# The last 512 columns of the second token tile as 384 and 128 instead of 256 and 256

## The chip, the cores and the metric

The kernel runs on one core of one Trainium2 chip. The core has a matrix engine (TensorE, in the profile PE, with its weight loads PEld), a vector engine (VectorE, DVE), a scalar engine (ScalarE, ACT), GpSimd (POOL) and a queue that issues transfers (SyncE, SP); each works through its own instructions in order and waits for the others by semaphores. The metric is the device time of one execution in microseconds, as the median of several runs.

## The reference

One layer of a decoder trunk on 256 tokens of width 2048, in float32. Cut to what the end of the kernel computes:

```python
h = rmsnorm(x, norm_mix_g)
u = h @ w_in                                   # 12 fields, 12288 columns
ya = b_g * causal_dwconv3(c_g * xa, conv_w) * silu(za)
...                                            # chunked gated recurrence -> yb
m = sigmoid(ga) * (ya @ w_a_out) + sigmoid(gb) * (yb @ w_b_out)
x = x + m @ w_o
gate = sigmoid(rmsnorm(x, ple_norm_g) @ w_ple_gate)
x = x + gate * (p @ w_ple_proj)
return rmsnorm(x, final_norm_g)
```

The change touches the last 512 columns of `gate`, the update of `x` by them, and the last norm.

## The kernel before

**Tiles.** The 256 tokens are two tiles of 128 (`NT` = 2, index `t`), which are the weights of the matmul (its 128 x 128 operand). The weight matrices of the layer are cut in groups of `CW` = 512 columns and stream through as the moving operand, so that one matmul gives 128 tokens x 512 columns, one PSUM bank. A float32 product is made of three: each operand is split into a rounded part and a rest (`hi` and `lo`, type fp32r), and `product` (line 954) issues hi x hi, hi x lo and lo x hi, each with its own weight load, all three added up in the same bank. Line 959 is the only matmul of all these products. The names in the profile: `xh`, `xl` are the two parts of the normed tokens, `whi`, `wlo` those of the weight matrix, `g` the PSUM bank.

**Order.** `steps` lists all groups of columns and, in each, the steps of K in pairs (`c`, two values of k each). For all groups but the last the loop over `steps[:last_group]` computes both tiles of tokens in step, into two banks. What follows a group on ScalarE, VectorE and GpSimd is a generator (an epilogue), and `advance` takes each active one a piece further after a step of the products.

**The last group.** The last 512 columns of the gate projection are done in another order (from line 1049): all 16 steps of K for the first tile of tokens, 512 columns wide; then all 16 for the second tile and columns 0 to 255 of the group; then all 16 for the second tile and columns 256 to 511. Each of the three has a bank of its own from a ring of four. The splits of the weights for all of them are kept, since they are used three times.

Behind each of the three comes its part of the last update:

- `last_half` (749) on 256 columns: sigmoid of the product times the token's scale on ScalarE (754), times the projection `pw` on VectorE (755), added to `x` (758), and square and sum over the columns on VectorE (759).
- `sums_so_far` (764), after the first of the two halves: adds what is known of the token's sum of squares (768, 772), so that only one number is left for the second half.
- `last_norm` (776), after the second: adds that number (779), takes the power -1/2 on GpSimd (780), scales all 2048 columns in pieces on ScalarE and VectorE (784, 786, 788) and stores them in three transfers on SP's queue (799).

For the first tile both halves come out of one product, and `ep_last` (801) runs all of this while the second tile's products go on. For the second tile `last_half` and `sums_so_far` of columns 0 to 255 lie beside the products of columns 256 to 511, and what follows these last products has nothing beside it.

Of the kernel before, what the change touches and what calls it, by code (L numbers as in the profile page):

```python
# [12 lines left out]
ALU = mybir.AluOpType  # L13
# [6 lines left out]
KT = D // P  # L20
# [3 lines left out]
CW = 512  # L24
PLE = 256
EPS = 1e-6

EARLY = {0: ((0, CW // 2), (CW // 2, CW), (CW, 2 * CW)), 1: ((0, CW), (CW, 2 * CW))}
WARM = (64,) * 51 + (CW,) * 3
LB_FLOOR = 1e-30  # L30
LB_MAX = 1.0 - 1e-6
# [15 lines left out]
def hybrid_kernel(ctx, tc, xT, x, pT, prm, gfin, masks, w_in, w_a, w_b, w_o, w_pg, w_pp, out):  # L47
# [24 lines left out]
    state = {"tmp": "tmp1"}  # L72
# [3 lines left out]
    def nm(s):  # L76
        uid[0] += 1
        return f"{s}_{uid[0]}"

    def t4(tag="t4", bufs=None):  # L80
        bufs = bufs or {"tmp1": 8, "tmp2": 5, "tmp3": 5}[state["tmp"]]
        return pools[state["tmp"]].tile([P, 1024], F32, tag=tag, bufs=bufs, name=nm(tag))

    def bank(tag):
        return ps.tile([P, CW], F32, tag=tag, bufs=4, name=nm(tag))
# [29 lines left out]
    def split(pos, c0=0, c1=2 * CW):  # L115
        w, g, c = stream[pos]
        src = load(pos)[:, pos % 2, :]

        pool, n = (pools["late"], 6) if (pos - state.get("late", len(steps))) % 10 < 6 and "late" in state else (wp, 4)
        if pos not in parts:  # L120
            parts[pos] = tuple(
                pool.tile([P, 2 * CW], F32R, tag=tag, bufs=n, name=nm(tag)) for tag in ("whi", "wlo")
            )
        hi, lo = parts[pos]
        s = slice(c0, c1)
        a = nc.scalar.activation(out=hi[:, s], in_=src[:, s], func=AF.Copy)  # L126
        v = nc.vector.tensor_tensor(  # L127
            out=lo[:, s], in0=src[:, s], in1=hi[:, s].bitcast(F32), op=ALU.subtract
        )
        state["splits"] = (a.ins, v.ins)  # L130
# [11 lines left out]
    active, done = [], 0  # L142
# [603 lines left out]
            d = xs[:, t, j * CW : (j + 1) * CW]  # L746
            nc.gpsimd.tensor_tensor(out=d, in0=d, in1=state["gfin"][:, j * CW : (j + 1) * CW], op=ALU.mult)

    def last_half(t, h, psum):

        xs, pw, ss, n = state["x"], state["pw", 3], state["ss3"], CW // 2
        gt = t4()[:, :n]
        d = xs[:, t, 3 * CW + h * n : 3 * CW + (h + 1) * n]
        nc.scalar.activation(out=gt, in_=psum, func=AF.Sigmoid, scale=state["rstd2"][:, t : t + 1])
        nc.vector.tensor_tensor(  # L755
            out=gt, in0=gt, in1=pw[:, t * CW + h * n : t * CW + (h + 1) * n], op=ALU.mult
        )
        nc.vector.tensor_tensor(out=d, in0=d, in1=gt, op=ALU.add)  # L758
        nc.vector.scalar_tensor_tensor(  # L759
            out=gt, in0=d, scalar=1.0 / D, in1=d, op0=ALU.mult, op1=ALU.mult,  # L760
            accum_out=ss[:, t * 6 + 3 + h : t * 6 + 4 + h],
        )

    def sums_so_far(t):

        tot = state["tot3", t] = sc(1, "tot3", 2)
        ss = state["ss3"]
        nc.vector.tensor_tensor(
            out=ss[:, t * 6 + 3 : t * 6 + 4], in0=ss[:, t * 6 + 3 : t * 6 + 4],
            in1=ss[:, t * 6 + 5 : t * 6 + 6], op=ALU.add,  # L770
        )
        nc.vector.tensor_reduce(
            out=tot, in_=ss[:, t * 6 : t * 6 + 4], axis=mybir.AxisListType.X, op=ALU.add
        )

    def last_norm(t):

        xs, r, tot = state["x"], sc(1, "r3", 2), state["tot3", t]
        nc.vector.tensor_tensor(out=tot, in0=tot, in1=state["ss3"][:, t * 6 + 4 : t * 6 + 5], op=ALU.add)
        nc.gpsimd.tensor_tensor(out=r, in0=tot, in1=mhalf[:, :1], op=ALU.pow)  # L780
        def scale(eng, c0, c1):
            d = xs[:, t, c0:c1]
            if eng is nc.scalar:
                nc.scalar.activation(out=d, in_=d, func=AF.Identity, scale=r)  # L784
            elif c0 < 3 * CW:
                nc.vector.tensor_scalar(out=d, in0=d, scalar1=r, scalar2=None, op0=ALU.mult)
            else:
                nc.vector.scalar_tensor_tensor(
                    out=d, in0=d, scalar=r, in1=state["gfin"][:, c0:c1], op0=ALU.mult, op1=ALU.mult
                )  # L790


        for pieces in (
            ((nc.vector, 768, 1024),), ((nc.scalar, 0, 512), (nc.vector, 512, 768)),
            ((nc.scalar, 1024, 1536), (nc.vector, 1536, 2048)),
        ):
            for eng, c0, c1 in pieces:
                scale(eng, c0, c1)
            nc.sync.dma_start(out=out[:, t, pieces[0][1] : c1], in_=xs[:, t, pieces[0][1] : c1])

    def ep_last(t, halves):

        last_half(t, 0, halves[0])
        sums_so_far(t)
        last_half(t, 1, halves[1])
        last_norm(t)
        yield

# [26 lines left out]
    wb = bank("s")  # L835
    for n in WARM:
        m = min(n, P)
# [104 lines left out]
    def advance():  # L942
        for e in list(active):
            step(e)
# [9 lines left out]
    def product(psum, op, k, t, hi, lo, first, last, which=(0, 1, 2)):  # L954

        oh, ol = (x[:, k, t * P : (t + 1) * P] for x in op)
        for n in which:
            a, b = ((oh, hi), (oh, lo), (ol, hi))[n]
            nc.tensor.matmul(psum, a, b, start=first and n == 0, stop=last and n == 2)  # L959

    psum = None
    for pos, (gi, c) in enumerate(steps[:last_group]):
        kind, j, w, g, opname = groups[gi]
# [9 lines left out]
        while done < min(pos + 1 + ahead(pos), len(steps)):  # L973

            for c0, c1 in EARLY.get(done, ((0, 2 * CW),)):
                if done == 0 and c0 % CW == 0:
# [22 lines left out]
        if c == 0:  # L999
            psum = [bank("s" if kind == "PP" and j > 1 else "g") for _ in range(NT)]  # L1000
        hi, lo = parts.pop(pos)
        for i in range(2):
            k = 2 * c + i
            for c0, c1 in EARLY[0][:2] if pos == 0 and i == 0 else ((0, CW),):
                s = slice(i * CW + c0, i * CW + c1)
# [41 lines left out]


    nlast = len(steps) - last_group
    for t, halves in ((0, (0, 1)), (1, (0,)), (1, (1,))):  # L1050
        bk, n = bank("g"), CW // 2
        for c in range(nlast):
            if done < len(steps):
                split(done)
                done += 1
            hi, lo = parts[last_group + c]
            for i in range(2):
                k = 2 * c + i
                s = slice(i * CW + halves[0] * n, i * CW + (halves[-1] + 1) * n)
                product(bk[:, : len(halves) * n], state["x1T"], k, t, hi[:, s], lo[:, s], k == 0, k == KT - 1)  # L1060
            if c % 2:
                advance()
        if t == 0:
            active.append(ep_last(t, [bk[:, h * n : (h + 1) * n] for h in halves]))
        else:
            last_half(t, halves[0], bk[:, :n])
            if halves[0] == 0:
                sums_so_far(t)
    last_norm(1)
    finish()  # L1070
# [74 lines left out]
```

## Time and profile before

| | us |
|---|---|
| median of 3 runs | 824.12 |
| lowest and highest | 823.97, 825.27 |
| the profiled execution, its own time | 824.47 |
| its span, first to last instruction | 822.7 |
| mean granted TensorE clock in it | 0.997 |

A row of a timeline is: start and length in us, engine, line, operation, the names of what it writes and reads, shapes, the count where rows are merged, and in brackets how long the engine stood idle before it and what ended that. In the groups by line, after the bar stand the busy time in us, the mean length of one in ns, and the idle time before. A matmul's record is longer than the distance to the next, because matmuls are pipelined; the distance from start to start is what one of them holds the engine.

### The profile page before, as it was taken

How to read it: one execution, taken by the hardware profiler on the slowest of the kernel's cores; microseconds unless marked ns; L12 is line 12 of the kernel's file. 1: busy time of each engine (PE TensorE's matmuls, PEld its weight loads, DVE VectorE, ACT ScalarE, POOL GpSimd, SP SyncE). 2: the span in 40 equal slices, each digit the busy share in tenths (PEclk: the TensorE clock that was granted, in tenths of full speed). 3: DMA queues.
4: the chain of work that ended last, by engine and by line, in shares of the span. 5: the costliest groups of instructions: out<-in, count | busy, mean ns of one | idle time of the engine just before them, and what ended most of it. 6: DMA issues, size and time to landing. Idle time of an engine off the chain costs nothing.

```text
span 822.7 us, 10783 instructions
## 1 busy us (share of the span) xinstructions
PE 813.4 (99%) x4235; PEld 676.0 (82%) x4236; DVE 531.1 (65%) x619; ACT 433.1 (53%) x559; POOL 90.6 (11%) x74
## 2 busy tenths in 40 slices
PE   9999999999999999999999999999999999999996
PEld 7888888888888888888888888888888888888885
DVE  5747698967766588877645546545545656679733
ACT  7666465565564565466443443544444455566522
POOL 1000045300000064200001001000100000001210
PEclk9999999999999999999999999999999999999998
DMA  9979656648776565748556755756755788887802
GB/s 339 368 271 340 222 188 209 214 155 253 259 230 229 198 205 165 246 153 294 198 184 184 264 189 173 252 205 205 239 182 195 253 278 275 314 291 279 301 0 104
DMA packets 41524, 187.27 MB, mean 228 GB/s; under 512 B 4736, under 2 KB 14208, under 8 KB 24320
## 3 DMA queue, kind: packets, MB, share of 16 engines
q1 hardware_dynamic: 41328, 186.31, 66.2%
q8 instruction: 33, 0.54, 0.3%
q10 hardware_dynamic: 144, 0.26, 0.1%
q14 instruction: 19, 0.16, 0.1%
HBM read 172.92 MB, written 13.63 MB: 227 GB/s over the span
## 4 chain that ended last, share of the span: by engine, by line
PE 97%; issue 1%; DMA 0%; DVE 0%; ACT 0%; ACTq 0%; POOLq 0%; POOL 0%
PE g L959 95%; PE s L959 1%; PE s L391 1%; DMA raw<-in_w_pp 0%; PE s L524 0%; PE s L547 0%; PE s L548 0%; PE s L546 0%; DVE t L755 0%; ACT xs L784 0%; DVE t L759 0%; DVE xs L758 0%; ACTq L1140 0%; POOLq L1140 0%; POOL r L780 0%
## 5 line engine op out<-in xcount | busy, mean ns | idle before, releaser
L127 DVE TENSOR_TENSOR wlo<-raw,whi 128x1024 fp32r<-128x1024 f32 (+1 forms) x295 | 368.0, 1252 | 252.1 <-ACT whi L126 251.5
L126 ACT ACTIVATE whi<-raw 128x1024 fp32r<-128x1024 f32 (+1 forms) x295 | 307.8, 1050 | 331.7 <-PE g L959 293.3
L959 PE MATMUL g<-whi,xl 128*128 128x512 f32 (+1 forms) x912 | 351.4, 385 | 0.0
L959 PE MATMUL g<-wlo,xh 128*128 128x512 f32 (+1 forms) x912 | 351.4, 385 | 0.0
L959 PE MATMUL g<-whi,xh 128*128 128x512 f32 (+1 forms) x912 | 351.2, 386 | 0.0
L959 PEld LDWEIGHTS g<-whi,xh 128*128 128x128 f32 x912 | 171.3, 188 | 34.4
L959 PEld LDWEIGHTS g<-whi,xl 128*128 128x128 f32 x912 | 171.3, 188 | 34.4
L959 PEld LDWEIGHTS g<-wlo,xh 128*128 128x128 f32 x912 | 171.3, 188 | 34.1
L959 PE MATMUL g<-whi,mh 128*128 128x512 f32 x128 | 49.8, 390 | 0.0
L959 PE MATMUL g<-wlo,mh 128*128 128x512 f32 x128 | 49.6, 389 | 0.0
L959 PE MATMUL g<-whi,ml 128*128 128x512 f32 x128 | 49.6, 390 | 0.0
L679 POOL TENSOR_TENSOR t<-ga,gb 128x512 f32<-128x512 f32 x6 | 10.6, 1792 | 198.3 <-DVE gb L674 198.3
L959 PE MATMUL g<-whi,yaTh 128*128 128x512 f32 (+1 forms) x74 | 28.3, 389 | 0.1
L959 PEld LDWEIGHTS g<-whi,mh 128*128 128x128 f32 x128 | 24.0, 188 | 5.2 <-ACT mh L685 0.3
L959 PEld LDWEIGHTS g<-whi,ml 128*128 128x128 f32 x128 | 23.9, 188 | 5.2 <-DVE ml L686 0.2
L959 PEld LDWEIGHTS g<-wlo,mh 128*128 128x128 f32 x128 | 24.0, 188 | 5.0
L959 PE MATMUL g<-whi,yaTl 128*128 128x512 f32 (+1 forms) x74 | 27.9, 384 | 0.0
L445 POOL TENSOR_TENSOR t<-b 128x512 f32<-128x512 f32 x10 | 20.4, 2037 | 68.5 <-DMA t<-turn 41.0
L959 PE MATMUL g<-wlo,yaTh 128*128 128x512 f32 (+1 forms) x74 | 27.9, 383 | 0.0
L959 PE MATMUL g<-whi,ybTh 128*128 128x512 f32 x64 | 24.9, 389 | 0.0
L959 PE MATMUL g<-wlo,ybTh 128*128 128x512 f32 x64 | 24.9, 389 | 0.0
L959 PE MATMUL g<-whi,ybTl 128*128 128x512 f32 x64 | 24.9, 389 | 0.0
(156 smaller groups left out, 518.2 us busy)
## 6 DMA issues: line engine op xcount, KB each, us to landing
raw<-in_w_in SPq DMA_DIRECT2D x85, 1024.0 KB, 5.0
raw<-in_w_o SPq DMA_DIRECT2D x16, 1024.0 KB, 5.6
raw<-in_w_pg SPq DMA_DIRECT2D x16, 1024.0 KB, 6.0
raw<-in_w_in SPq DMA_DIRECT2D x22, 512.0 KB, 7.9
turn<-t SPq DMA_DIRECT2D x72, 128.0 KB, 2.6
t<-turn SPq DMA_DIRECT2D x18, 512.0 KB, 5.3
raw<-in_w_a SPq DMA_DIRECT2D x8, 1024.0 KB, 5.3
raw<-in_w_b SPq DMA_DIRECT2D x8, 1024.0 KB, 5.2
```

What stands on the lines that cost most here:

```text
L126: a = nc.scalar.activation(out=hi[:, s], in_=src[:, s], func=AF.Copy)
L127: v = nc.vector.tensor_tensor(out=lo[:, s], in0=src[:, s], in1=hi[:, s].bitcast(F32), op=ALU.subtract)
L391: nc.tensor.matmul(heads(bk)[r, h, c if at is None else slice(at, at + 32)], key(h)[:, r], query(h)[:, c], start=True, stop=True, tile_pos ...
L445: nc.gpsimd.tensor_tensor(out=er, in0=br, in1=ref, op=ALU.subtract)
L679: (nc.vector if j == 3 else nc.gpsimd).tensor_tensor(out=spread(m, t), in0=blocks(ga[:, s]), in1=blocks(gb[:, s]), op=ALU.add)
L959: nc.tensor.matmul(psum, a, b, start=first and n == 0, stop=last and n == 2)
```

## The change

The constant `LAST` = 128 sets the width of the last part of the second tile. `last_half`, which took the number of a half, becomes `last_part`, which takes the columns `c0` to `c1`. The loop at the end takes the ranges of columns: 0 to 512 for the first tile, then 0 to 384 and 384 to 512 for the second. The first tile's update is still made in two halves of 256.

```diff
+LAST = 128
...
-    def last_half(t, h, psum):
+    def last_part(t, h, c0, c1, psum):

-        xs, pw, ss, n = state["x"], state["pw", 3], state["ss3"], CW // 2
-        gt = t4()[:, :n]
-        d = xs[:, t, 3 * CW + h * n : 3 * CW + (h + 1) * n]
+        xs, pw, ss = state["x"], state["pw", 3], state["ss3"]
+        gt = t4()[:, : c1 - c0]
+        d = xs[:, t, 3 * CW + c0 : 3 * CW + c1]
         nc.scalar.activation(out=gt, in_=psum, func=AF.Sigmoid, scale=state["rstd2"][:, t : t + 1])
         nc.vector.tensor_tensor(
-            out=gt, in0=gt, in1=pw[:, t * CW + h * n : t * CW + (h + 1) * n], op=ALU.mult
+            out=gt, in0=gt, in1=pw[:, t * CW + c0 : t * CW + c1], op=ALU.mult
         )
...
-    def ep_last(t, halves):
+    def ep_last(t, psum):

-        last_half(t, 0, halves[0])
+        last_part(t, 0, 0, CW // 2, psum[:, : CW // 2])
         sums_so_far(t)
-        last_half(t, 1, halves[1])
+        last_part(t, 1, CW // 2, CW, psum[:, CW // 2 :])
         last_norm(t)
...
-    for t, halves in ((0, (0, 1)), (1, (0,)), (1, (1,))):
-        bk, n = bank("g"), CW // 2
+    for t, c0, c1 in ((0, 0, CW), (1, 0, CW - LAST), (1, CW - LAST, CW)):
+        bk = bank("g")
...
-                s = slice(i * CW + halves[0] * n, i * CW + (halves[-1] + 1) * n)
-                product(bk[:, : len(halves) * n], state["x1T"], k, t, hi[:, s], lo[:, s], k == 0, k == KT - 1)
+                s = slice(i * CW + c0, i * CW + c1)
+                product(bk[:, : c1 - c0], state["x1T"], k, t, hi[:, s], lo[:, s], k == 0, k == KT - 1)
...
-            last_half(t, halves[0], bk[:, :n])
-            if halves[0] == 0:
+            last_part(t, int(c0 > 0), c0, c1, bk[:, : c1 - c0])
+            if c0 == 0:
                 sums_so_far(t)
```

More of the change, by code (lines that the diff above doesn't have):

```diff
@@ L1063, in hybrid_kernel @@
         if t == 0:
-            active.append(ep_last(t, [bk[:, h * n : (h + 1) * n] for h in halves]))
+            active.append(ep_last(t, bk))
         else:
-            last_half(t, halves[0], bk[:, :n])
-            if halves[0] == 0:
+            last_part(t, int(c0 > 0), c0, c1, bk[:, : c1 - c0])
+            if c0 == 0:
                 sums_so_far(t)
```

## The prediction

> **What bounds the kernel now.** I read the page's head first, then the chain that ended last.
>
> ```profile
> span 822.7 us, 10783 instructions
> PE 813.4 (99%) x4235; PEld 676.0 (82%) x4236; DVE 531.1 (65%) x619; ACT 433.1 (53%) x559; POOL 90.6 (11%) x74
> PE 97%; issue 1%; DMA 0%; DVE 0%; ACT 0%; ACTq 0%; POOLq 0%; POOL 0%
> 359.48 443.62 PE g L959 x1956
> ```
>
> TensorE is busy from end to end and makes up 97% of the chain (the last row is one piece of that chain: 1956 matmuls, all 512 columns wide, 443.62 us long). So one matmul of 512 columns holds TensorE for 443.62 / 1956 = 0.2268 us from its start to the start of the next. Whatever the change does to the sum of these gaps goes straight into the span; whatever it does behind the last matmul goes there too, because nothing else runs by then.
>
> Next I read the end of the span, engine by engine in equal stretches of the last product (columns after the stretch: PE, weight loads PEld, DVE, ACT, POOL, granted clock, DMA share, GB/s), and the timeline where the two 256-column halves of the second tile begin and end.
>
> ```profile
> 802.92:808.70 5.78, 5.78 (x50) 5.78 (x49) 3.81 (x14) 2.18 (x4) 0.55 (x1) 1.00 0.09 27
> 808.67:814.43 5.76, 5.76 (x50) 5.71 (x48) 1.60 (x6) 0.48 (x1) 0.00 (x0) 1.00 0.41 161
> 802.92 0.28 PE L959 MATMUL g<-whi,xh 128*128 128x256 f32 x1
> ...
> 808.67 0.28 PE L959 MATMUL g<-whi,xh 128*128 128x256 f32 x1
> ...
> 814.31 0.28 PE L959 MATMUL g<-whi,xl 128*128 128x256 f32 x1
> L959 PE MATMUL g<-whi,xl 128*128 128x512 f32 x880 | 342.4, 389 | 0.0
> L959 PE MATMUL g<-whi,xl 128*128 128x256 f32 x32 | 9.1, 283 | 0.0
> ```
>
> Each half is 48 matmuls (16 steps of K by three products). The first of the 96 starts at 802.92 and the last at 814.31, so one of 256 columns takes 11.39 / 95 = 0.1199 us. The granted clock is 1.00 in both stretches. The last two rows, from the groups by line with shapes kept apart, give the recorded length of one: 389 ns and 283 ns. These are longer than the gaps because a matmul's record includes its drain.
>
> Two things are to be seen. First, from 512 to 256 columns the gap falls by 0.1069 us, or 0.418 ns a column, and 0.013 us are left that don't depend on the width. Secondly, in these two stretches the weight loads are as busy as the matmuls (5.78 of 5.78, 5.71 of 5.76), while over the whole span they are at 82%: with 256 columns the loads have no air left.
>
> Last, the tail behind the last matmul:
>
> ```profile
> 808.93 0.48 ACT L754 ACTIVATE t<-g,r2r 128x256 f32<-128x256 f32 x1 [0.70 <-PE g L959]
> ...
> 814.63 0.47 ACT L754 ACTIVATE t<-g,r2r 128x256 f32<-128x256 f32 x1 [5.22 <-PE g L959]
> 815.13 0.42 DVE L755 TENSOR_TENSOR t<-t,pw 128x256 f32<-128x256 f32 x1 [3.95 <-ACT t L754]
> 815.59 0.42 DVE L758 TENSOR_TENSOR xs<-xs,t 128x256 f32<-128x256 f32 x1
> 816.05 0.42 DVE L759 SCALAR_TENSOR_TENSOR t<-xs 128x256 f32<-128x256 f32 x1
> 816.40 0.08 DVE L759 DVE_READ_ACCUMULATOR t<-xs 128x1 f32 x1
> 816.52 0.16 DVE L779 TENSOR_TENSOR tot<-tot,ss 128x1 f32<-128x1 f32 x1
> 816.76 0.55 POOL L780 TENSOR_TENSOR r<-tot,mhalf 128x1 f32<-128x1 f32 x1 [9.89 <-DVE tot L779]
> 817.34 1.34 ACT L784 ACTIVATE xs<-xs,r 128x512 f32<-128x512 f32 x2 [2.24 <-POOL r L780]
> ```
>
> Sigmoid, multiply, add, square and sum, total, power, scale, store: each waits for the one before (the first row is the sigmoid of the half before, at 808.93, which lies beside the matmuls). The first four work on the width of the last part. What stands from 816.52 on has fixed sizes and moves as a block with whatever comes before it.
>
> **The change part by part.**
>
> *The 48 wider matmuls.* They grow from 256 to 384 columns. No row shows 384; the bounds are 0.1199 and 0.2268 us, and by the straight line between them it is 0.1734. I take that, since every count of columns seen so far only adds its 0.418 ns. Cost: 48 x 0.0535 = +2.57 us.
>
> *The 48 narrower matmuls.* They shrink from 256 to 128 columns, and each still has a 128 x 128 weight load of its own (4236 loads to 4235 matmuls in the page's first rows), also the second product of a K step, which has the same tokens as weights as the first. No row shows a matmul of this split kind with fewer than 256 columns. The lowest price is the straight line: 0.013 + 128 x 0.000418 = 0.0665 us, which would give the 2.57 us back exactly. But these rows, the only places where two such loads follow each other with nothing in front of them, speak against it:
>
> ```profile
> 345.60 0.19 PEld L959 LDWEIGHTS g<-whi,xh 128*128 128x128 f32 x1
> 345.60 0.50 PE L959 MATMUL g<-whi,xh 128*128 128x512 f32 x1
> 345.71 0.19 PEld L959 LDWEIGHTS g<-wlo,xh 128*128 128x128 f32 x1
> 345.94 0.40 PE L959 MATMUL g<-wlo,xh 128*128 128x512 f32 x1
> ...
> 318.53 0.19 PEld L959 LDWEIGHTS g<-whi,xh 128*128 128x128 f32 x1
> 318.64 0.19 PEld L959 LDWEIGHTS g<-wlo,xh 128*128 128x128 f32 x1
> ```
>
> After another kind of work has ended, the second load starts 0.11 us after the first, and not sooner. The second matmul starts at 345.94, so by the gap of 0.2268 the first really began to stream at 345.71, 0.11 us after its load began and when the next load began. So a load holds its place for 0.11 us, and the next one begins when the matmul that uses it begins. With 256 columns (0.107 us of columns) this is just hidden; with 128 columns (0.053 us) it isn't, and the load sets the pace. A second kind of matmul with 128 columns and full weights bounds it too:
>
> ```profile
> 358.81 0.22 PE s L546 x2
> 359.03 0.22 PE s L547 x2
> 358.87 0.39 PE L547 MATMUL s<-v,aoff 128*128 128x128 f32 x2
> ```
>
> The plain f32 products of the recurrence are two records each, 0.22 us for both, 0.1115 us a record, each with a load of its own. So the narrow gap lies between 0.1115 (this row) and 0.1199 (own kind at 256 columns, as if nothing were saved by the narrower width). I take 0.115, between the two, nearer to the rows in which the load alone is seen.
>
> The stream from 802.92 to the end of the last record was 11.39 + 0.283 = 11.67 us. It becomes 48 x 0.1734 + 47 x 0.115 + 0.230 (the recorded length at 128 columns by the line through 389 and 283) = 8.32 + 5.41 + 0.23 = 13.96 us: **+2.28 us**, with +2.12 and +2.52 at the two ends.
>
> The Trainium skill, "TensorE: Matmul & The Clock Gate", section "LDWEIGHTS (loading the stationary operand)", speaks against this change too: a load takes its number of columns divided by 1.2 ns, 107 ns here, however many columns the matmul streams. The rows above agree (0.11). By the page's figure the stream would grow by 1.90 us in place of 2.28.
>
> *The tail.* The four width-bound steps go from 256 to 128 columns.
>
> ```profile
> L738 DVE TENSOR_TENSOR t<-t,pw 128x512 f32<-128x512 f32 x6 | 4.1, 692 | 4.2 <-ACT t L735 4.2
> L755 DVE TENSOR_TENSOR t<-t,pw 128x256 f32<-128x256 f32 x4 | 1.6, 426 | 14.0 <-ACT t L754 14.0
> L754 ACT ACTIVATE t<-g,r2r 128x256 f32<-128x256 f32 x4 | 1.8, 473 | 13.4 <-PE g L959 13.4
> L558 ACT ACTIVATE t<-s,r1r 128x128 f32<-128x128 f32 x16 | 5.6, 362 | 2.2 <-PE s L546 2.2
> L788 DVE SCALAR_TENSOR_TENSOR xs<-xs,r,gfin_t 128x512 f32<-128x512 f32 x2 | 1.5, 742 | 0.0
> ```
>
> VectorE: (692 - 426) / 256 = 1.04 ns a column, so 0.133 us less for each of three instructions, 0.40 us. ScalarE: 473 to 362 ns, 0.11 us. Together **-0.51 us**. The bounds are close: a VectorE instruction on one column (L779, 0.16) against one of 256 (0.42) gives 1.02 ns a column, so -0.50; the steeper line from L759 to L788 (742 against 421 ns) gives -0.59.
>
> *What moves and costs nothing.* The same sigmoid, multiply, add and square on the first part are half as wide again and start later, at 802.92 + 8.3 + drain = about 811.4 rather than 808.93. ScalarE needs some 0.58 us, VectorE three times 0.56 and the two small sums 0.35, so they are done at about 814.1. What hides them is the second part's matmuls; VectorE is wanted again at 816.9 + 0.4 = 817.3. Were the narrow matmuls as cheap as 0.0665 us, VectorE would be wanted at 815.0, still 0.9 us later. The count of matmuls, loads, banks and stores stays; no wait is added, nothing goes past another instruction on SP's or POOL's queue; the three stores of the second tile move with the scale that they wait for.
>
> *The sum.* +2.28 - 0.51 = +1.77 us, against the profiled execution's 824.47 us (its span of 822.7 and 1.8 around it): 826.24. That execution was 0.35 above the median of 824.12, so on the median: **825.9 us**, +0.21%. With both ends: +2.12 - 0.59 = +1.5 to +2.52 - 0.50 = +2.0, so 825.6 to 826.1, or 825.3 to 826.5 with the scatter of the runs shown.
>
> **The rivals.**
>
> *Narrow products fall to the plain f32 rate.* The f32 products above need 0.223 us for 128 columns (two records), that is 1.74 ns a column, while the split kind has 0.44 at 512 columns. No row shows that the split kind keeps its rate below 256 columns; that no part of this kernel goes narrower with it leaves the case open. If a narrow product is worked at the f32 rate, whatever the reason, the stream is 8.32 + 47 x 0.223 + 0.39 (length of such a pair) = 19.19 us, +7.52; less 0.51, +7.0: 831.1 us, +0.85%. Against it: the recorded kind is the same with the same load, and at 256 columns no step is seen. Chance 0.27.
>
> *The load hides after all (not slower).* If the next load could be started as early as wanted, the narrow gap is 0.0665 us, the stream 11.68 us, +0.01, and only the tail's gain stays: -0.5 us, 823.6. It decides from a load that takes its place for less than 0.067 us. For it speaks one row:
>
> ```profile
> 317.24 1.25 PEld L391 LDWEIGHTS s<-X 128*32 128x32 f32 x128 [0.35 <-issue]
> ```
>
> Loads of 32 columns follow each other every 0.010 us there, or 0.04 for 128 columns, so loading isn't slow in itself. Against it: those go to four separate strips of the array, while full loads keep 0.11 us wherever they are seen. Chance 0.10.
>
> *Loads overlap in part.* A load's record is 0.19 us long and the next starts 0.11 us after, so two are under way at once; with short matmuls in between the overlap could grow. Halfway between 0.0665 and 0.1115, a gap of 0.089 gives 8.32 + 4.18 + 0.23 = 12.73, +1.06; less 0.51, +0.55: 824.7. The same page of the Trainium skill, section "Back-to-back issue gap", has a stream of load and matmul pairs at about 81 ns for 128 columns, which would give +0.69 - 0.51 = +0.18, or 824.3. Its figure beside that for 512 columns is 131 ns, and the trace disagrees (226.8), so I give this little weight. Chance 0.07.
>
> **How the numbers follow.** Forecast 0.56, f32 rate 0.27, hidden load 0.10, partial overlap 0.07. The predicted time is the forecast's, 825.9. The range runs from 825.0, below the forecast's own 825.3, up to 831.3, over the f32 case; it leaves out the two cheap cases, 0.17. A change within 0.2% (1.65 us, 822.5 to 825.8) is about what a measurement of this kernel can tell from none. The forecast lies at this line: of its 0.56 I count 0.35 above and 0.21 below. Slower 0.35 + 0.27 = 0.62; same 0.21 + 0.07 + 0.08 = 0.36; faster 0.02, should the hidden load meet a larger gain in the tail.
>
> **What would show it.** In the profile of the changed kernel: 48 matmuls of 384 columns 0.173 us apart; then 48 of 128 columns, 0.11 to 0.12 us apart with the weight loads as densely packed, 0.22 for the f32 rate (perhaps as 96 records), 0.067 for the hidden load. The sigmoid at the very end should be at 0.36 us and the VectorE instructions at 0.29. The prediction is wrong if the narrow gap is under 0.10 or over 0.13 us, if the wide gap isn't 0.173, or if VectorE is still at work on the first part when the last sigmoid is done.

## The result and the profile after

| | before | after |
|---|---|---|
| median of 14 runs, us | 824.25 | 826.07 |
| ratio of the times, 95% interval | | 1.0020 (1.0012 to 1.0029) |
| profiled execution, us | 824.47 | 826.07 |
| its span, us | 822.7 | 824.3 |

The changed kernel is slower by 1.8 us between the medians (1.6 us between the profiled executions). The interval lies wholly above 1, and the ratio is just at the 0.2% line. One of the 14 executions of the changed kernel took 1181.36 us, at a mean granted clock of 0.653, and is left out of the ratio.

These are rows of the changed kernel's timeline, where the 384-column matmuls end and the 128-column ones begin and end (TensorE and its weight loads; the lines of the code have moved by one).

```profile
802.88 0.33 PE L960 MATMUL g<-whi,xh 128*128 128x384 f32 x1
...
811.05 0.33 PE L960 MATMUL g<-whi,xl 128*128 128x384 f32 x1
811.06 0.19 PEld L960 LDWEIGHTS g<-whi,xh 128*128 128x128 f32 x1
811.23 0.22 PE L960 MATMUL g<-whi,xh 128*128 128x128 f32 x1
811.23 0.19 PEld L960 LDWEIGHTS g<-wlo,xh 128*128 128x128 f32 x1
811.29 0.27 PE L960 MATMUL g<-wlo,xh 128*128 128x128 f32 x1
811.34 0.19 PEld L960 LDWEIGHTS g<-whi,xl 128*128 128x128 f32 x1
811.40 0.28 PE L960 MATMUL g<-whi,xl 128*128 128x128 f32 x1
...
816.42 0.28 PE L960 MATMUL g<-whi,xl 128*128 128x128 f32 x1
```

The wide matmuls are (811.05 - 802.88) / 47 = 0.174 us apart. By the starts of the records the first narrow one takes only 0.06 us (811.23 to 811.29), but it was no cheaper than the others: the load for the second begins at 811.23, and the next load at 811.34, 0.11 us later. From the second on, the record of a narrow matmul begins 0.06 us after its own load does, while that load still holds its place, and is 0.27 or 0.28 us long where the first one's is 0.22. So these records begin about 0.05 us ahead of the streaming. The 45 gaps from 811.40 to 816.42 are 0.1116 us each, with a load begun every 0.11 us.

The busy time of the engines in the two stretches (TensorE, weight loads, VectorE, ScalarE, GpSimd, granted clock, DMA share, GB/s):

```profile
802.88:811.23 8.35, 8.35 (x50) 8.35 (x49) 3.81 (x14) 2.18 (x4) 0.55 (x1) 1.00 0.31 116
811.23:816.42 5.19, 5.19 (x48) 5.19 (x48) 2.00 (x6) 0.58 (x1) 0.00 (x0) 1.00 0.06 21
```

Both stretches are full of matmul and of load records, and the clock is 1.00. Busy shares can't tell here which of the two sets the pace; the distance between starts, against the width, can.

The tail of the changed kernel:

```profile
814.08 0.16 DVE L773 TENSOR_REDUCE tot<-ss 128x1 f32<-128x4 f32 x1
816.74 0.37 ACT L755 ACTIVATE t<-g,r2r 128x128 f32<-128x128 f32 x1 [4.67 <-PE g L960]
817.13 0.29 DVE L756 TENSOR_TENSOR t<-t,pw 128x128 f32<-128x128 f32 x1 [2.90 <-ACT t L755]
817.46 0.29 DVE L759 TENSOR_TENSOR xs<-xs,t 128x128 f32<-128x128 f32 x1
817.79 0.29 DVE L760 SCALAR_TENSOR_TENSOR t<-xs 128x128 f32<-128x128 f32 x1
818.00 0.08 DVE L760 DVE_READ_ACCUMULATOR t<-xs 128x1 f32 x1
818.12 0.16 DVE L780 TENSOR_TENSOR tot<-tot,ss 128x1 f32<-128x1 f32 x1
```

The first row is the last instruction of the 384-column update. It is over 2.9 us before VectorE is wanted again, so the wider first update is hidden. From the sigmoid to the last sum it is 818.12 - 816.74 = 1.38 us, against 816.52 - 814.63 = 1.89 before.

The balance: the stream from the first matmul of the second tile to the end of the last one's record is 816.42 + 0.275 - 802.88 = 13.82 us against 11.67, **+2.14**; the tail is **-0.51**; together +1.63. The whole stretch, from the first matmul of the second tile to the end of the span, is 824.3 - 802.88 = 21.42 us against 822.7 - 802.92 = 19.78, +1.64. So within the 0.1 us to which the span is given, the stream and the tail are the whole change.

### The profile page after: what moved, and what is told of

The parts are those of the page before. It is cut to its first block, busy times and chain, and to the rows that moved or that the text cites. A ratio compares the mean times of both kernels' runs of the same rounds, so it can differ in the third digit from the quotient of the medians.

```text
span 824.3 us, 10783 instructions
## 1 busy us (share of the span) xinstructions
PE 815.2 (99%) x4235; PEld 678.1 (82%) x4236; DVE 531.4 (64%) x619; ACT 432.9 (53%) x559; POOL 90.6 (11%) x74
## 4 chain that ended last, share of the span: by engine, by line
PE 97%; issue 1%; DMA 1%; DVE 0%; ACT 0%; ACTq 0%; POOLq 0%; POOL 0%
PE g L960 95%; PE s L960 1%; PE s L392 1%; DMA raw<-in_w_pp 1%; PE s L525 0%; PE s L548 0%; PE s L549 0%; PE s L547 0%; DVE t L756 0%; ACT xs L785 0%; DVE t L760 0%; DVE xs L759 0%; ACTq L1141 0%; POOLq L1141 0%; POOL r L781 0%
## 5 line engine op out<-in xcount | busy, mean ns | idle before, releaser
L960 PE MATMUL g<-wlo,xh 128*128 128x512 f32 (+2 forms) x912 | 352.4, 386 | 0.0
L960 PE MATMUL g<-whi,xl 128*128 128x512 f32 (+2 forms) x912 | 352.4, 386 | 0.0
L960 PE MATMUL g<-whi,xh 128*128 128x512 f32 (+2 forms) x912 | 352.2, 387 | 0.0
```

## The experiments

The loss could have been the load of the weights (theory) or a slower matmul below 256 columns: at half the rate 128 columns take 0.107 us, and with a rest of about 0.004 us (as the expectations below take it; with the 0.013 of the wide matmuls it would be 0.120) that is 0.111 too. As long as that rest is unknown, the two can't be told apart at 128 columns. Four widths, a smaller load, and each half of the change alone were run. In the table the stretch runs from the first matmul of the second tile to the end of the span of the profiled execution; it leaves out the beginning of the kernel, whose length differs from one execution to the next (this first matmul starts between 802.7 and 805.0 us). The span is given to 0.1 us only.

| widths | stretch, us | narrow gap, us | time, us |
|---|---|---|---|
| 256 + 256 (before) | 19.78 | 0.120 | 824.25 |
| 272 + 240 | 19.55 | 0.112 | 824.30 (11 runs; before 824.53 beside it) |
| 320 + 192 | 20.37 | 0.111 | 825.49 (one run) |
| 384 + 128 (after) | 21.42 | 0.112 | 826.07 |
| 416 + 96 | 21.86 | 0.112 | 826.53 (one run) |
| 448 + 64 | 23.81 | 0.112, then 0.214 | 828.46 (one run) |
| 448 + 64 again | 23.29 | 0.112, then 0.213 | 828.92 (3 runs) |

### Widths 192 and 240

```diff
-LAST = 128
+LAST = 192
```

> 320 and 192 columns. Theory: the narrow gap is again 0.111 us, because 0.013 + 192 x 0.000418 = 0.093 is still below the load's 0.111; wide gap 0.147; stream 7.04 + 0.09 + 46 x 0.1115 + 0.28 = 12.5 us, 0.9 more than before, tail 0.25 less; time about 824.9. Rival (half rate below 256): narrow gap 0.165, stream 15.1, time about 827.4.

The wide and the narrow matmuls of this kernel, first and last of 48 each:

```profile
803.33:810.36 7.03, 7.03 (x49) 7.03 (x48) 3.82 (x14) 2.18 (x4) 0.55 (x1) 1.00 0.23 83
810.36:815.59 5.23, 5.23 (x49) 5.23 (x48) 1.80 (x6) 0.53 (x1) 0.00 (x0) 1.00 0.24 95
```

The windows run from the first wide to the first narrow matmul (48 gaps of 0.146 us) and from there to the last narrow one (47 gaps of 0.111). At 192 columns the pace is the same as at 128, and half rate (0.165) is excluded. The stretch grew by 0.59 us, where 0.9 - 0.25 = 0.65 was expected. The time of this one run, 825.49, missed its 824.9 by 0.6; here the second tile's first matmul starts at 803.33, 0.4 us later than before.

```diff
-LAST = 128
+LAST = 240
```

> 272 and 240 columns. Theory: the load is just hidden at 0.013 + 240 x 0.000418 = 0.113 us, so the two gaps (0.1266 and 0.113) add up to the 0.2398 of before and the stream is the same; the tail is 16 columns shorter, 0.06 us less: 824.2, not to be told from before by time. Rival (half rate below 256): narrow gap 0.20 us, 4.4 us more: 828.6.

```profile
803.45:809.46 6.01, 6.01 (x49) 6.01 (x48) 3.82 (x14) 2.18 (x4) 0.55 (x1) 1.00 0.10 31
809.46:814.71 5.25, 5.25 (x50) 5.25 (x48) 1.65 (x6) 0.49 (x1) 0.00 (x0) 1.00 0.44 171
```

Again windows from first to first and from first to last: gaps of 0.125 and 0.112 us, in sum 0.237 where 0.240 was expected. The stretch is 0.23 us shorter than before in this one profile, but the ratio of the times is 1.0001 (0.9992 to 1.0010): not to be told from before. The half rate (828.6) is excluded here as well. No step stands at 256 columns; the pace bends near 240, where the columns need what the load needs.

### Widths 96 and 64

> The second tile's last 512 columns as 448 and 64. Theory (the load of the 128 x 128 weights takes its place for 0.11 us and sets the pace): the 64-column matmuls stay 0.111 us apart, as at 128; the wide ones need 0.013 + 448 x 0.000418 = 0.200. Stream 48 x 0.200 + 0.06 + 46 x 0.1115 + 0.28 = 15.1 us, 3.4 more than before; tail 0.76 less; time about 826.9. Rival (below 256 columns the matmul itself runs at half its rate, 0.84 ns a column): narrow gap 0.058, stream 12.5, time about 824.3.

```diff
-LAST = 128
+LAST = 64
```

The gap was the theory's at first and then doubled. Rows of its timeline, where that happens, and the two stretches of narrow matmuls:

```profile
812.65 0.27 PE L960 MATMUL g<-wlo,xh 128*128 128x64 f32 x1
...
816.34 0.28 PE L960 MATMUL g<-wlo,xh 128*128 128x64 f32 x1
816.45 0.33 PE L960 MATMUL g<-whi,xl 128*128 128x64 f32 x1
816.59 0.40 PE L960 MATMUL g<-whi,xh 128*128 128x64 f32 x1
816.80 0.40 PE L960 MATMUL g<-wlo,xh 128*128 128x64 f32 x1
...
818.94 0.40 PE L960 MATMUL g<-whi,xl 128*128 128x64 f32 x1
```

```profile
812.65:816.45 3.80, 3.80 (x37) 3.80 (x35) 2.20 (x6) 0.63 (x1) 0.00 (x0) 1.00 0.01 2
816.59:818.94 2.35, 2.35 (x14) 2.35 (x13) 0.00 (x0) 0.00 (x0) 0.00 (x0) 0.50 0.00 0
```

From 812.65 to 816.34 there are 33 gaps of 0.112 us at clock 1.00, as at 128 and 192 columns: a matmul of 64 columns takes no less than one of 192. From 816.59 to 818.94 there are 11 gaps of 0.214 us at clock 0.50. The clock's fall costs about 12 x 0.10 = 1.2 us, which is most of why the time was 828.5 and not 826.9. Whether it was chance, and whether 96 columns suffer it, was asked next.

> 448 and 64 columns once more. Theory: the clock falls to 0.50 again about 3.9 us after the first narrow matmul, gaps double from 0.111 to 0.213 us, and the time is again near 828.4. Rival (chance): clock 1.00 to the end, about 1.1 us less.

> 416 and 96 columns. Theory on the pace: narrow gap 0.111 us again. Theory on the clock (the granted clock fell to 0.50 in the 64-column part 3.9 us after its first matmul, because the columns fill only 0.027 of each 0.111 us, 24%, while at 128 columns, 48%, it stayed at 1.00): at 96 columns, 36%, either the clock stays, and the stretch from the first wide matmul to the end is about 19.78 + 2.76 - 0.64 = 21.9 us, or it falls as at 64 columns, for the last 12 to 15 matmuls, and the stretch is 23.1 to 23.4. Rival (the fall at 64 columns was a chance event): clock 1.00 here and in the repeat at 64.

```diff
-LAST = 128
+LAST = 96
```

The repeat, in windows of one microsecond around the fall:

```profile
816.00:817.00 1.00, 1.00 (x10) 1.00 (x10) 0.00 (x0) 0.00 (x0) 0.00 (x0) 0.93 0.00 0
817.00:818.00 1.00, 1.00 (x6) 1.00 (x6) 0.00 (x0) 0.00 (x0) 0.00 (x0) 0.50 0.00 0
```

It fell again, 4.4 us after the first narrow matmul where it had been 3.9, and the three runs gave 828.92, 0.52% over before (0.36 to 0.68). So it isn't chance. At 96 columns the gap was 0.112, and the clock fell just as the last matmul ran:

```profile
816.80:817.00 0.20, 0.20 (x5) 0.20 (x3) 0.00 (x0) 0.00 (x0) 0.00 (x0) 1.00 0.00 0
817.00:817.10 0.10, 0.10 (x3) 0.10 (x2) 0.00 (x0) 0.00 (x0) 0.00 (x0) 0.97 0.00 0
817.10:817.20 0.10, 0.10 (x2) 0.03 (x1) 0.00 (x0) 0.00 (x0) 0.00 (x0) 0.50 0.00 0
```

It cost nothing any more: the stretch of 21.86 is what was expected with the clock kept. So the clock falls at 96 columns too, 5.3 us after the first narrow matmul, when the last one is all but done.

The 3.9, 4.4 and 5.3 us are no measure of what the clock bears. In the eleven profiles it stays at 1.00 for 808.96, 812.37 or 815.79 us from its rise to its fall, whatever the kernel; these are 237, 238 and 239 times 3.4133 us, so in these traces it falls only at the end of a step of 3.41 us. At 64 and 96 columns it fell at the end of the first step that narrow matmuls filled (813.12 to 816.53, 813.44 to 816.86 and 813.68 to 817.10). At 128 columns two kernels have such a step, and both kept the clock after it: 811.81 to 815.22 in the second form of the products alone below, and this one in the first form, with the step behind it:

```profile
813.53:816.94 3.41, 3.41 (x33) 3.41 (x32) 0.63 (x4) 0.00 (x0) 0.00 (x0) 1.00 0.00 0
816.94:820.36 3.42, 1.15 (x11) 1.01 (x10) 1.44 (x5) 0.47 (x1) 0.10 (x1) 1.00 0.00 0
```

In the changed kernel the narrow matmuls fill no whole step. Whether the clock would fall after several full steps at 128 columns wasn't tried.

### Half the weights

```diff
-                product(bk[:, : c1 - c0], ..., k == KT - 1)
+                m = 64 if c0 and 0 < k < KT - 1 else P
+                product(bk[:m, : c1 - c0], ..., k == KT - 1, m=m)
```

> 384 and 128 columns, but in the narrow part's K steps 1 to 14 only tokens 0 to 63 of the tile are loaded as weights (64 columns of weights in place of 128; the products of tokens 64 to 127 for these steps are left out). The matmuls still stream 128 columns. Theory: a load of 64 columns takes about half as long, so these 42 matmuls fall to what their columns need, 0.0665 us: 42 x 0.045 = 1.9 us less than the changed kernel, about 824.2. Rival (half rate below 256 columns, or a fixed price for each pair of load and matmul): the gap stays at 0.111 and the time at 826.1.

```profile
813.49 0.27 PE L960 MATMUL g<-whi,xl 128*128 128x128 f32 x1
813.60 0.23 PE L960 MATMUL g<-whi,xh 128*64 128x128 f32 x1
813.66 0.22 PE L960 MATMUL g<-wlo,xh 128*64 128x128 f32 x1
...
816.06 0.22 PE L960 MATMUL g<-whi,xl 128*64 128x128 f32 x1
816.12 0.27 PE L960 MATMUL g<-whi,xh 128*128 128x128 f32 x1
816.23 0.28 PE L960 MATMUL g<-wlo,xh 128*128 128x128 f32 x1
```

The columns streamed are the same 128. With 64 columns of weights the matmuls are (816.06 - 813.60) / 41 = 0.060 us apart, and with the full weights behind them at once 0.11 again. So the pace hangs on the size of the load, and not on a rate of the matmul or a fixed price of a pair. With half the weights a matmul also gives half the rows of results, and no run changes the load without them. That two full loads are 0.11 us apart in front of 512-column matmuls too, in the prediction's rows at 318.53 and 318.64, speaks for the load. The stretch, from 804.97 to 824.2, is 19.23 us, 2.19 less than the changed kernel's (1.9 expected). The time, 825.99, missed its expectation of 824.2, because this execution began late: the 528 matmuls that start at 16.73 before start at 18.77 here.

```profile
18.77 119.68 PE g L960 x528
```

### Each half alone

The first form of the products alone put both parts into one bank.

```diff
-        bk = bank("g")
+        bk = bank("g") if c0 == 0 else bk
...
-            last_part(t, int(c0 > 0), c0, c1, bk[:, : c1 - c0])
+            u0, u1 = (CW // 2, CW) if c0 else (0, CW // 2)
+            last_part(t, int(c0 > 0), u0, u1, bk[:, u0:u1])
```

> The matmuls as 384 and 128 columns, into one bank, but the last updates of the second tile as before, in halves of 256 columns behind the first and the second of the two. Theory: the stream's whole loss without the tail's gain, 2.15 us by the trace of the changed kernel: 824.25 + 2.15 = 826.4, 0.26% over before. Rival (the loss comes from elsewhere, such as the longer update of 384 columns): no more than the changed kernel's own 826.07, or less.

It gave 827.75, ratio 1.0037 (1.0024 to 1.0051), more than either expected, and its timeline says why:

```profile
811.55 0.34 PE L960 MATMUL g<-whi,xl 128*128 128x384 f32 x1
811.99 0.47 ACT L755 ACTIVATE t<-g,r2r 128x256 f32<-128x256 f32 x1 [3.29 <-PE g L960]
812.51 0.19 PEld L960 LDWEIGHTS g<-whi,xh 128*128 128x128 f32 x1 [0.94 <-ACT t L755]
812.52 0.33 PE L960 MATMUL g<-whi,xh 128*128 128x128 f32 x1 [0.62 <-ACT t L755]
```

The first narrow matmul waited for the sigmoid that read other columns of the same bank: it starts 0.97 us after the last wide one where 0.17 was due, 0.80 too late. The experiment had brought a wait of its own. (The stretch is 826.2 - 803.38 = 22.82 us, +3.04: 2.24 beside this wait.) So it was made again with two banks.

```diff
+            psum = twice[:, :LAST].rearrange("p (n c) -> p n c", n=1).to_broadcast([P, 2, LAST])
         nc.scalar.activation(out=gt, in_=psum, func=AF.Sigmoid, scale=state["rstd2"][:, t : t + 1])
```

> The matmuls as in the changed kernel, in two banks, so that the first narrow matmul waits for nothing. The last update is 256 columns wide again: its sigmoid reads the 128 columns of the narrow part's bank twice, so that columns 256 to 383 of the second tile get the gate of columns 384 to 511. Theory: from the first matmul of the wide part to the end of the span 19.78 us before become 21.93, the loss of the stream (2.15) without the tail's gain; time 2.15 over before, 826.5. Rival (the 2.24 that the first form showed beside its wait are the loss, or the update of 384 columns costs something): 22.02 or more, or 21.42 as in the changed kernel.

826.62 us, ratio 1.0026 (1.0015 to 1.0036): 2.2 us over its before of 824.44. The stretch is 825.1 - 803.24 = 21.86 us, +2.08, the expected 21.93 within the rounding of the span.

```diff
-LAST = 128
+LAST = 256
...
-            last_part(t, int(c0 > 0), c0, c1, bk[:, : c1 - c0])
+            u0 = c0 + 128 if c0 else 0
+            last_part(t, int(c0 > 0), u0, c1, bk[:, u0 - c0 : c1 - c0])
```

> The matmuls in halves of 256 columns as before; the update of columns 256 to 383 of the second tile is left out (gate, sum into x and their squares), so that what follows the last matmul is 128 columns wide. Theory: the tail's gain alone, 0.51 us: 823.7. Rival (part of the tail's gain is taken back in the scale and the stores): 824.0 or more.

823.92 us against 824.42 beside it, ratio 0.9993 (0.9985 to 1.0002); by times alone it can't be told from no change. The stretch is 822.6 - 803.32 = 19.28 us, -0.50, and the sum of the two halves, +2.08 - 0.50 = +1.58, is the change's +1.64 within the rounding.

## Why the prediction was right

- *The wide gap*: 0.1734 taken from the line between 256 and 512 columns, 0.1738 measured.
- *The narrow gap*: 0.115 taken, between 0.1115 and 0.1199; 0.1116 measured, the lower end. That end came from the plain f32 products and from two loads with nothing in front of them; the upper one, the gap of the own kind at 256 columns, lay too high. That the load sets the pace was argued in the prediction from these few rows; the widths of 64 to 192 columns at one and the same gap, and half the weights at about half the gap (0.060), show it.
- *The loads at 256 columns.* The prediction took their full busy share as a sign that they have no air left. By the spacing that is nearly so (0.1116 of 0.1199 us), but the share doesn't show it: a load's record is 0.19 us long, so the records fill the time at every shorter gap, and in the 384-column stretch too (8.35 of 8.35 us at 0.174 us a matmul).
- *The stream* came to +2.14, where +2.28 was forecast. The term that was too large is the narrow gap, by 47 x 0.0034 = 0.16. That the first narrow matmul seems to take 0.06 us by the starts, and that the last record is longer than counted (0.275 us, not 0.230), are the same 0.05 us seen at both ends, and almost cancel.
- *The tail*: -0.51 forecast and measured, down to the instruction: 0.37 us for the sigmoid (0.362 from the row with 128 columns), 0.29 for each VectorE instruction.
- *What hides the first update*: it was to end at about 814.1 and ended at 814.24; VectorE was wanted again at 817.13 (817.3 forecast).
- *The sum*: +1.77 forecast; +1.64 in the profile's stretch, +1.82 between the medians, which have an interval of 1.0 to 2.4 us. That the medians come so near the forecast is in part luck, since by the profile the sum was 0.13 too large.
- *The rivals*: the f32 rate (gap 0.223) and the hidden load (0.0665) both fall with the measured gap. Of the partial overlap (0.089) nothing is left either. The figure of the Trainium skill, "TensorE: Matmul & The Clock Gate", section "Back-to-back issue gap", 81 ns for a pair with 128 columns, does not hold for this kind of operand (112 ns measured). The estimate by the Trainium skill's section "LDWEIGHTS (loading the stationary operand)" on the same page, 128 / 1.2 = 107 ns for 128 columns of weights, agrees but for 5 ns.

## What to carry to other kernels

In these runs no matmul that brought its own weights was cheaper than their load. So compare the width it streams with the columns of weights it loads, and expect the gap to stop shrinking where the two meet (here at about 240 columns against 128 columns of weights, 0.11 us). A shorter last piece shortens the tail by its width, but is paid for on every step of K; here 0.51 us were bought for 2.14. Where two explanations give the same time at one size, run other sizes.

## What was not expected of the hardware

- **The clock falls under a busy engine.** In the 64-column part the matmul and load records fill the time, and still the granted clock fell from 1.00 to 0.50; 64 columns at 0.418 ns are 0.027 us of each 0.112, 24%. With 96 columns (36%) it fell after a filled step too, with 128 (48%) it did not. The two levels are those that the Trainium skill names in "TensorE: Matmul & The Clock Gate", Part 1 on the clock gate (full and half rate); it has the gate close after an idle window of about 3.4 us. That length agrees with the steps of 3.41 us, but these runs show the clock fall with no idle time between matmuls. What is counted in a step of 3.41 us these runs don't settle. A low share of streaming columns fits all of them. The busy time of the records does not: the changed kernel kept its clock after the step from 813.79 to 817.20, in which TensorE is busy for 2.91 us, and the 96-column kernel lost it after one that was busy throughout. If it is the share of columns, the limit lies between 35% (30 starts of 96 columns in that step, clock lost) and 38% (24 starts of 128, clock kept), an estimate from these two steps.
- **The pace that the load sets follows that clock**: 0.112 us at 1.00, 0.214 us at 0.50.
- **The fixed part of a matmul's gap is no constant.** 0.013 us stand beside the columns at 256 and 512 columns with 128 columns of weights, but with 64 columns of weights 128 columns took 0.060 us, 0.006 more than their 128 x 0.418 ns = 0.0535. Half of the full load's 0.1116 is 0.056, so whether the columns or the smaller load set these 0.060 us is open.
